# A decoder block with a mixture of experts on one core: weight runs of 8 KB, transposes of strided columns, an input norm on VectorE, and a convolution norm cut into groups of eight transposes

## The chip, the core and the metric

The kernel runs on one core of a Trainium2 chip. The engines of that core are named as in the profile: PE is TensorE, PEld its weight loads, DVE is VectorE, ACT is ScalarE, POOL is GpSimd, and SP is SyncE, whose queue starts most of the DMAs. The metric is the time of one execution on the device, in microseconds (us). Before the change it is 1435.72 us, the median of three runs that lie between 1428.46 and 1436.32 us.

## What is computed

The input `x` has 1024 tokens of 1024 features, all in float32. The block has two mixers on the same normed input, a gate for each, and behind them 32 experts of which every token takes two.

```python
h = rms_norm(x, attn_norm_g)
proj = jnp.matmul(h, w_in)                       # 1024 -> 4608 columns
...
conv_out = conformer_conv(u_conv, ...)           # 31 taps, layer_norm over 512 channels, silu
attn_out = diff_attention(q, k, v, lam, ...)     # 4 heads, causal
merged = (gates[:, :, 0] * jnp.matmul(conv_out, w_conv_out)
          + gates[:, :, 1] * jnp.matmul(attn_out, w_attn_out))
x = x + jnp.matmul(merged, w_out)
h2 = rms_norm(x, ffn_norm_g)
# group of 8 experts by argmax, the two best in it, rows sorted by expert
hid = jax.nn.silu(jnp.matmul(xb, w_g[e])) * jnp.matmul(xb, w_u[e])     # 1024 -> 512
y = jnp.matmul(hid, w_d[e]) * wb[:, None]                              # 512 -> 1024
x = x + scatter_add(y)
```

## The kernel before

Every float32 operand of a large matmul is split into a high and a low part (`split`: ACT copies to the high part, DVE subtracts for the low part, both at lines 93 and 94 of a shared helper), and `mm3` makes three matmuls of each product (lines 98, 99 and 100).

**Prologue and attention (0 to 325 us).** A loop over U goes through 4 heads and 8 blocks of 128 tokens. The order of PE and ACT in it is written out by hand; a string of characters (`plan`) sets where the eight steps of a projection, the transposes of the next token block (`p` and `P`) and the attention steps of earlier blocks stand. In the first eight turns the blocks of `x` are also normed and transposed. SP loads a block into one of four slots of `xts`; ACT sums its squares (`prep_a`), DVE makes 1/sqrt from that (`rsqrt`, lines 65 to 75, ten short instructions); POOL multiplies the block by the norm's weights `gb` (`prep_g`, line 202); DVE multiplies the identity by the 1/sqrt of each token (`prep_s`, line 207); and PE multiplies the block by that diagonal, which transposes and scales it in one (`prep_b`, line 218). The result is split into `hTh` and `hTl`. The low parts of the first head's weights (`wla`) are made by DVE for two chunks and by POOL for two (`wsplit`).

**Merge (325 to 665 us).** Gates are made one after the other, 24 matmuls each (`gate`), with the convolution's taps on DVE between them. The convolution's output is normed over channels in three steps: `norm_stats` (16 transposes, ACT copies them out of PSUM at line 616, DVE makes mean and variance), `norm_silu` (16 transposes back, and for each 512 columns ACT makes a sigmoid at line 635 and an affine copy at line 637) and `norm_split`. Each is done once for each half of the tokens. `merge_conv` puts them between gates by its table `steps`: `norm_stats(0)`, then `norm_silu(0)` with `norm_stats(1)` directly behind it, then `norm_silu(1)`.

**Output projection and routing (665 to 824 us).** For each half of the columns and each token block, PE makes 24 matmuls; DVE adds `x` (line 801); `scaled` multiplies by the second norm's weights on POOL (`uu`, line 815); and ACT's queue stores that to `h2d` in DRAM, from which the experts gather rows. `scaled` permutes in the same step: within every 512 columns element 4p+k goes to place 128k+p, by reads 16 bytes apart. On ACT the store stands ahead of `h2T` (line 865), the copy of a transposed block that PE's logits (`pl`, line 874) need. DVE splits the next block of the merged mixers meanwhile (`ml`, line 94). In the second half, after every second block and at the end, `route` runs a chain of short DVE instructions and small matmuls (`oh`, `ohb`, then `pr` on PE at line 961).

**Experts (824 to 1419 us).** Each of 32 experts has six chunks of 1 MB of weights, which SP loads into a ring of 12 buffers `ra`, with at most five loads in flight (`chunk_dma`). A chunk of the gate or up weights gives each partition one run of 8 KB; a chunk of the down weights gives it two runs of 4 KB. POOL gathers the expert's rows (`gx`, line 1002), PE transposes them (8 transposes in `x_front`, line 1013) and the hidden rows (4 in `hid_t`, line 1041), makes 72 matmuls of 128x512, and POOL adds the result into the output (line 1055).

## Time and profile before

| | |
|---|---|
| median of the runs | 1435.72 us |
| the profiled execution | 1441.21 us, of which the span of instructions is 1439.5 us |
| busy share of the span | PE 94%, PEld 79%, DVE 76%, ACT 55%, POOL 17% |
| granted clock of PE, mean | 0.975 of full speed |
| DMA | 264.81 MB, 184 GB/s over the span |
| chain that ended last | PE 39%, issue 31%, DMA 11%, DVE 7%, POOL 7%, ACT 3% |

The profiled execution is slower than the median by 5.5 us, 0.4%, and 1.7 us of its time lie outside the span. A busy PE is not PE at its peak: its matmuls overlap, and the starts of neighbouring ones say more than their durations.

### The profile page before, as it was taken

To read this page: it belongs to the slowest core of one execution; us is meant where nothing else is said; L and a number is where in the kernel's file an instruction comes from. 1 tells how busy PE (TensorE), PEld (TensorE's weight loads), DVE (VectorE), ACT (ScalarE), POOL (GpSimd) and SP (SyncE) were. 2 spreads that over 40 slices of the span, in tenths; PEclk is the share of its full clock that TensorE was granted. 3 is DMA by queue.
4 is the path that set the end of the run, shared out by engine and by line. 5 is a ranking of instruction groups with operands and counts; after the bars stand their busy time and mean duration, and the time that the engine had idled before them with its cause. 6 is when DMAs were issued, how large, how long until landed. Compare 5 with 4: busy or idle time off the path is not lost.

```text
span 1439.5 us, 18415 instructions
## 1 busy us (share of the span) xinstructions
PE 1349.0 (94%) x6854; PEld 1136.7 (79%) x6854; DVE 1087.7 (76%) x1402; ACT 788.2 (55%) x1109; POOL 240.6 (17%) x349
## 2 busy tenths in 40 slices
PE   5899999999999999899988589999999999999995
PEld 5899999888888888778767468888888887777774
DVE  7776776645789895565575869999998888888893
ACT  4466675653111112531342258888888777777782
POOL 4322121200000000000232211111111212222211
PEclk9999999999999999999997889999999999999997
DMA  5110100102111121043942189999999999999981
GB/s 180 35 45 12 34 18 18 30 27 77 51 44 40 49 59 44 1 130 117 325 158 96 48 297 352 358 371 377 363 370 368 366 368 360 359 361 362 349 326 17
DMA packets 105789, 264.81 MB, mean 184 GB/s; under 512 B 14033, under 2 KB 59234, under 8 KB 89314
## 3 DMA queue, kind: packets, MB, share of 16 engines
q1 hardware_dynamic: 89218, 237.73, 44.8%
q0 software_dynamic: 9216, 16.81, 4.8%
q10 hardware_dynamic: 7264, 9.08, 1.8%
q8 instruction: 55, 0.90, 0.2%
q14 instruction: 36, 0.29, 0.1%
HBM read 255.18 MB, written 25.17 MB: 195 GB/s over the span
## 4 chain that ended last, share of the span: by engine, by line
PE 39%; issue 31%; DMA 11%; DVE 7%; POOL 7%; ACT 3%; POOLq 0%; SPq 0%; ACTq 0%; DVEq 0%
DMA out_dram<-y,idx 8%; PE pg L99 4%; PE pg L98 4%; PE pg L100 4%; POOL out_dram L1055 3%; POOL gx L1002 2%; PE pq L98 2%; PE pq L100 2%; PE pq L99 2%; PE po L363 2%; PE pc L98 2%; PE pc L100 2%; PE pc L99 2%; PE pb L98 2%; PE pb L99 2%
## 5 line engine op out<-in xcount | busy, mean ns | idle before, releaser
L94 DVE TENSOR_TENSOR cl<-ra,ch 128x2048 fp32r<-128x2048 f32 x192 | 436.1, 2289 | 69.6 <-ACT ch L93 69.0
L93 ACT ACTIVATE ch<-ra 128x2048 fp32r<-128x2048 f32 x192 | 365.2, 1920 | 94.7 <-DMA ra<-in_w_gate_e_dram 39.1
L99 PE MATMUL pg<-cl,xh 128*128 128x512 f32 x512 | 203.8, 398 | 4.8 <-DVE cl L94 4.8
L98 PE MATMUL pg<-ch,xh 128*128 128x512 f32 x512 | 203.8, 398 | 3.7 <-ACT ch L93 2.1
L100 PE MATMUL pg<-ch,xl 128*128 128x512 f32 x512 | 201.8, 394 | 0.1
L597 DVE SCALAR_TENSOR_TENSOR ac<-yy,dw,ac 128x1024 f32<-128x1024 f32 x120 | 153.1, 1283 | 2.3
L99 PEld LDWEIGHTS pg<-cl,xh 128*128 128x128 f32 x512 | 96.9, 189 | 27.1 <-DVE cl L94 7.5
L98 PEld LDWEIGHTS pg<-ch,xh 128*128 128x128 f32 x512 | 97.2, 190 | 26.1 <-ACT ch L93 4.1
L100 PEld LDWEIGHTS pg<-ch,xl 128*128 128x128 f32 x512 | 96.9, 189 | 20.5 <-DVE xl L94 0.9
L98 PE MATMUL py<-ch,dh 128*128 128x512 f32 x256 | 103.0, 402 | 1.9 <-ACT dh L93 1.9
L1055 POOL DMA_INDIRECT out_dram<-y,idx x32 | 66.0, 2063 | 226.1 <-ACT y L1054 202.8
L99 PE MATMUL py<-cl,dh 128*128 128x512 f32 x256 | 101.5, 397 | 0.0
L100 PE MATMUL py<-ch,dl 128*128 128x512 f32 x256 | 101.3, 396 | 0.0
L98 PE MATMUL pg<-hTh,whb 128*128 128x512 f32 x256 | 100.1, 391 | 0.0
L100 PE MATMUL pg<-hTh,wlb 128*128 128x512 f32 x256 | 99.8, 390 | 0.0
L99 PE MATMUL pg<-hTl,whb 128*128 128x512 f32 x256 | 99.8, 390 | 0.0
L1002 POOL DMA_INDIRECT gx<-h2d,idx x32 | 53.9, 1685 | 265.5 <-PE pt L1013 226.1
L98 PE MATMUL pq<-wha,hTh 128*128 128x384 f32 x256 | 95.7, 374 | 0.0
L100 PE MATMUL pq<-wha,hTl 128*128 128x384 f32 x256 | 86.8, 339 | 0.8 <-DVE hTl L94 0.8
L93 ACT ACTIVATE whb<-wrb 128x512 fp32r<-128x512 f32 x48 | 30.0, 631 | 104.3 <-PE pg L99 86.1
L99 PE MATMUL pq<-wla,hTh 128*128 128x384 f32 x256 | 86.9, 339 | 0.0
L332 ACT ACTIVATE ee<-sc,mx 128x128 f32<-128x128 f32 (+7 forms) x64 | 47.1, 745 | 22.5 <-DVE mx L330 22.5
(308 smaller groups left out, 2766.3 us busy)
## 6 DMA issues: line engine op xcount, KB each, us to landing
ra<-in_w_gate_e_dram SPq DMA_DIRECT2D x64, 1024.0 KB
ra<-in_w_up_e_dram SPq DMA_DIRECT2D x64, 1024.0 KB
ra<-in_w_down_e_dram SPq DMA_DIRECT2D x64, 1024.0 KB
wrb<-in_w_in_dram SPq DMA_DIRECT2D x32, 256.0 KB
wra<-in_w_in_dram SPq DMA_DIRECT2D x32, 192.0 KB
xts<-in_x_dram SPq DMA_DIRECT2D x8, 512.0 KB
wrb<-in_w_in_dram SPq DMA_DIRECT2D x32, 128.0 KB
wor<-in_w_out_dram SPq DMA_DIRECT2D x8, 512.0 KB
```

The lines of the kernel that those rows point to most:

```text
L93: self.nc.scalar.activation(hi, src, AF.Copy)
L94: self.last_split = (eng or self.nc.vector).tensor_tensor(lo, src, hi.bitcast(F32), op=ALU.subtract).ins
L98: mm(ps, lhsT=lh, rhs=rh, start=first, stop=False)
L99: mm(ps, lhsT=lh, rhs=rl, start=False, stop=False)
L100: mm(ps, lhsT=ll, rhs=rh, start=False, stop=last)
L332: nc.scalar.activation(ee[:, :n], sc[:, :n], AF.Exp, bias=mx, accum_out=s["sm"][qb][:, c:c + 1])
L363: nc.tensor.matmul(po, lhsT=s["at"][j // 4][:, j % 4], rhs=s["V"][j], start=j == 0, stop=j == qb)
L597: nc.vector.scalar_tensor_tensor(ac, yy[:, j:j + T], w(j), ac, op0=ALU.mult, op1=ALU.add)
L1002: self.nc.gpsimd.indirect_dma_start(out=gx, out_offset=None, in_=self.h2d, in_offset=bass.IndirectOffsetOnAxis(ap=idx, axis=0), bounds_che ...
L1055: nc.gpsimd.indirect_dma_start(out=self.out, out_offset=bass.IndirectOffsetOnAxis(ap=idx, axis=0), in_=y, in_offset=None, bounds_check=T - ...
```

## The change

There are four parts.

- **Prologue.** `prep_g` is one DVE instruction, `scalar_tensor_tensor`, that multiplies a block in place by its 1/sqrt and by `gb` (in two pieces for the first two blocks). POOL's multiply and the diagonal are gone, and `prep_b` transposes against the constant identity. There are five slots for `x` instead of four, the order of the first loads differs, and DVE makes the low parts of all four weight chunks. The first two turns of the loop have plans of their own.
- **Convolution norm.** `norm_stats` and `norm_silu` are cut in two, eight transposes each, and each piece stands behind a gate of its own; the last two stand in the loop that projects the convolution's output.
- **Stored rows.** `scaled` is gone: DVE multiplies 512 contiguous columns (`uu`), and rows are stored unpermuted. `x_front` now picks every fourth element of a gathered row, 16 bytes apart, as the operand of its transposes.
- **Down weights.** They are loaded as one run of 8 KB for each partition, and `hid_t` picks every second element, 8 bytes apart, for its transposes.

A fallback loop for experts with more than 128 rows has the same edit of its weight loads; it is not shown.

```diff
@@ -181,9 +181,12 @@
+    def xslot(self, tb):
+        return self.xmisc[:, 3] if tb == 4 else self.xts[:, tb if tb < 4 else tb - 5]
+
...
     def prep_g(self, tb):
-        xt = self.xts[:, tb % 4]
-        self.xg[tb] = xg = xt if tb else self.xmisc[:, 3]
-        self.nc.gpsimd.tensor_tensor(xg, xt, self.gb, op=ALU.mult)
-
-    def prep_s(self, tb):
-        c = (tb % 2) * P
-        self.dg[tb] = dg = self.xmisc[:, 3, c:c + P] if tb else self.xmisc[:, 2, 7 * P:]
-        self.nc.vector.tensor_scalar(dg, self.ident, self.xr[tb], None, op0=ALU.mult)
+        w = D // 2 if tb < 2 else D
+        for c in range(0, D, w):
+            x = self.xslot(tb)[:, c:c + w]
+            g = self.nc.vector.scalar_tensor_tensor(x, x, self.xr[tb], self.gb[:, c:c + w], op0=ALU.mult, op1=ALU.mult)
+        return g.ins
@@ -215,8 +215,7 @@
         for k in range(4):
-            nc.tensor.matmul(pt[:, k], lhsT=self.xg[tb][:, (kk + k) * P:(kk + k + 1) * P], rhs=self.dg[tb],
-                             start=True, stop=True)
+            nc.tensor.transpose(pt[:, k], self.xslot(tb)[:, (kk + k) * P:(kk + k + 1) * P], self.ident)
@@ -402,30 +401,28 @@
             self.xload(0)
+            wload(0, 0)
             nc.sync.dma_start(self.gb, row_bcast(i["attn_norm_g"], D))
-            wload(0, 0)
+            wload(0, 1)
             self.xload(1)
-            wload(0, 1)
             wload(0, 2)
             self.xload(2)
+            self.xload(3)
             wload(0, 3)
-            self.xload(3)
+            self.xload(4)
             self.consts_load()
-            self.xr, self.xg, self.dg = {}, {}, {}
-            self.prep_g(0)
+            self.xr = {}
             self.prep_a(0)
-            self.prep_s(0)
+            with tc.issue_after(self.prep_g(0)):
+                wsplit(0, 0)
+            self.prep_b(0, 0)
+            wsplit(0, 1)
+            self.prep_b(0, 4)
             self.prep_a(1)
+            wsplit(0, 2)
             self.prep_g(1)
...
-            wsplit(0, 3, nc.gpsimd)
+            wsplit(0, 3)
+            self.prep_a(2)
...
@@ -490,12 +485,15 @@
                 plan = "0p12cP3a4qk56Q7" if nxt else "012c3a4qk5Q67"
+                if U < 2:
+                    plan = ("012345p67P", "0123p45P67")[U]
...
                         if U == 0:
+                            self.prep_g(2)
                             self.prep_a(3)
                             self.prep_g(3)
@@ -603,29 +601,32 @@
-    def norm_stats(self, th):
+    def norm_stats(self, th, u):
...
-        for t, zt in enumerate(zs):
+        for t in (2 * u, 2 * u + 1):
...
-    def norm_silu(self, th):
+    def norm_silu(self, th, u):
...
-        for cb in range(NCB):
+        for cb in (2 * u, 2 * u + 1):
@@ -693,26 +694,30 @@
+    def norm_step(self, n, steps):
+        if n in steps:
+            f, th, u = steps[n]
+            f(th, u)
+            if (f, th, u) == (self.norm_silu, 1, 1):
+                self.norm_split(1)
+
     def merge_conv(self, fills, stop, steps):
...
+        order = [(j, th) for j in range(ND - 2) for th in range(2)]
+        order += [(j, th) for th in range(2) for j in (ND - 2, ND - 1)]
+        for n, (j, th) in enumerate(order):
...
+            self.gate(Wg[j], th, s2[th][:, j])
...
+            self.norm_step(n, steps)
+            if (j, th) == (ND - 1, 0):
                 self.norm_split(0)
...
             for j in range(ND):
                 if th == 0 and j + 2 < ND:
                     Wo.append(wload(j + 2))
-                if (th, j) == (0, 2):
-                    self.norm_split(1)
                 pb = self.branch(Wo[j], self.hTh[:, :NCB], self.hTh[:, NCB:], th)
                 sg, mg = s2[th][:, j], self.mg[th][:, j]
                 nc.vector.tensor_tensor(sg, pb, sg, op=ALU.mult)
                 nc.vector.tensor_tensor(mg, mg, sg, op=ALU.add)
+                if th == 0:
+                    self.norm_step(16 + j, steps)
@@ -803,16 +808,12 @@
                 uu = ep.tile([P, 512], F32, name="uu", bufs=2)
-                self.scaled(uu, xt, gb2)
+                nc.vector.tensor_tensor(uu, xt, gb2, op=ALU.mult)
                 nc.scalar.dma_start(self.h2d[sl, ns], uu)
...
-    def scaled(self, uu, xt, gb2):
-        by = lambda a: a.rearrange("t (p k) -> t k p", k=4)
-        self.nc.gpsimd.tensor_tensor(uu.rearrange("t (k p) -> t k p", k=4), by(xt), by(gb2), op=ALU.mult)
@@ -1009,8 +1010,9 @@
             pt = self.ps.tile([P, 4, P], F32, name="pt", tag="T", bufs=2)
+            g = gx[:, k0 * P:(k0 + 4) * P].rearrange("t (p k) -> t k p", k=4)
             for k in range(4):
-                nc.tensor.transpose(pt[:, k], gx[:, (k0 + k) * P:(k0 + k + 1) * P], self.ident)
+                nc.tensor.transpose(pt[:, k], g[:, k], self.ident)
@@ -1038,7 +1040,8 @@
                 c = q * w + k
-                nc.tensor.transpose(pt[:, k], sg[:, c * P:(c + 1) * P], self.ident)
+                g = sg[:, c // 2 * 2 * P:(c // 2 + 1) * 2 * P].rearrange("t (p k) -> t k p", k=2)
+                nc.tensor.transpose(pt[:, k], g[:, c % 2], self.ident)
@@ -1082,10 +1083,9 @@
-        wd = i["w_down_e"][0, e].rearrange("(k p) f -> p k f", p=P)
...
-                [self.chunk_dma(wd[:, k:k + 2]) for k in (0, 2)])
+        wd = i["w_down_e"][0, e].rearrange("(c p k) f -> c p (k f)", p=P, k=2)
+        return ([self.chunk_dma(wg[c], F) for c in range(2)], [self.chunk_dma(wu[c], F) for c in range(2)],
+                [self.chunk_dma(wd[c], D) for c in range(2)])
@@ -1256,8 +1255,9 @@
-        b.merge_conv(6, 4, {4: [(b.norm_stats, 0)], 5: [(b.norm_silu, 0), (b.norm_stats, 1)],
-                            ND - 1: [(b.norm_silu, 1)]})
+        b.merge_conv(6, 4, {8: (b.norm_stats, 0, 0), 9: (b.norm_stats, 0, 1), 11: (b.norm_silu, 0, 0), 12: (b.norm_silu, 0, 1),
+                            13: (b.norm_stats, 1, 0), 14: (b.norm_stats, 1, 1), 17: (b.norm_silu, 1, 0),
+                            19: (b.norm_silu, 1, 1)})
```

What DVE does at the first token block, as it stands in DVE's order (`rr` is the 1/sqrt, `xmisc` the diagonal and, in the new kernel, `gb`). Before:

```order
L75 SCALAR_TENSOR_TENSOR rr<-xn1t,xn1y 128x1
L207 TENSOR_SCALAR xmisc<-ident,rr 128x128
L65 TENSOR_SCALAR xn1v<-ss 128x1
L66 TENSOR_SCALAR xn1y<-xn1v 128x1
L67 TENSOR_SCALAR xn1y<-xn1y 128x1
L68 TENSOR_SCALAR xn1v<-xn1v 128x1
L71 TENSOR_SCALAR xn1t<-xn1y,xn1v 128x1
L94 TENSOR_TENSOR wla<-wra,wha 128x768
L75 SCALAR_TENSOR_TENSOR xn1y<-xn1t,xn1y 128x1
```

After, at the same place, with the buffers' numbers:

```order
L75 SCALAR_TENSOR_TENSOR rr_128<-xn1t_132,xn1y_131 128x1
L206 SCALAR_TENSOR_TENSOR xts_84<-xts_84,rr_128,xmisc_85 128x512 x2
L94 TENSOR_TENSOR wla_146<-wra_92,wha_145 128x768
L94 TENSOR_TENSOR hTl_80<-pt_149,hTh_79 128x4x128
L94 TENSOR_TENSOR wla_157<-wra_96,wha_156 128x768
L94 TENSOR_TENSOR hTl_80<-pt_160,hTh_79 128x4x128
L65 TENSOR_SCALAR xn1v_170<-ss_167 128x1
L66 TENSOR_SCALAR xn1y_171<-xn1v_170 128x1
L67 TENSOR_SCALAR xn1y_171<-xn1y_171 128x1
```

The diagonal has become a multiply of the whole block in two pieces, and two splits of weights and both splits of the transposed first block now stand ahead of the second block's 1/sqrt.

What DVE does where the first routing meets the end of a token block (`wro` takes the sum with `x`, `oh` and `ohb` are the routing's one-hot tables that PE waits for). Before:

```order
L801 TENSOR_TENSOR wro<-wro,px 128x512
L954 CAST ef<-ei 128x4
L966 TENSOR_TENSOR dl<-e_6975 128x2
L972 TENSOR_REDUCE gs<-ge 128x2
L956 TENSOR_TENSOR oh<-io_6342,ef 128x128
L957 TENSOR_TENSOR ohb<-oh 128x64
L969 TENSOR_TENSOR rh<-oh,idm 128x4x32
L971 TENSOR_TENSOR rh<-oh,rr 128x4x32
L979 TENSOR_TENSOR ev<-oh,pr 128x128
L94 TENSOR_TENSOR ml<-mg_4025,mh 128x1024
L981 TENSOR_REDUCE slot<-ev 128x4
L983 TENSOR_TENSOR S<-io_6342,slot 128x512
```

After:

```order
L806 TENSOR_TENSOR wro<-wro,px 128x512
L954 MAX_INDEX ei<-e_6969,off 128x8 x2
L811 TENSOR_TENSOR uu<-wro,gb_6784 128x512
L955 CAST ef<-ei 128x4
L967 TENSOR_TENSOR dl<-e_6969 128x2
L973 TENSOR_REDUCE gs<-ge 128x2
L957 TENSOR_TENSOR oh<-io_6336,ef 128x128
L94 TENSOR_TENSOR ml<-mg_4019,mh 128x1024
L958 TENSOR_TENSOR ohb<-oh 128x64
L970 TENSOR_TENSOR rh<-oh,idm 128x4x32
L972 TENSOR_TENSOR rh<-oh,rr 128x4x32
L980 TENSOR_TENSOR ev<-oh,pr 128x128
```

The multiply `uu` has come into DVE's order ahead of the tables, and the split `ml` of the next block has moved from behind them to between `oh` and `ohb`.

What PE does around the second place of the convolution norm (`pg` is a gate, `pt<-ident,yy` belongs to `norm_silu` and `pt<-ident,ac` to `norm_stats`). Before:

```order
L99 MATMUL pg<-hTl,whb 128x512
L100 MATMUL pg<-hTh,wlb 128x512
L632 MATMUL pt<-ident,yy 128x128 x16
L615 MATMUL pt<-ident,ac 128x128 x16
L98 MATMUL pg<-hTh,whb 128x512
L99 MATMUL pg<-hTl,whb 128x512
```

After, at the first piece of `norm_silu`:

```order
L98 MATMUL pg<-hTh,whb 128x512
L99 MATMUL pg<-hTl,whb 128x512
L100 MATMUL pg<-hTh,wlb 128x512
L633 MATMUL pt<-ident,yy 128x128 x8
L98 MATMUL pg<-hTh,whb 128x512
L99 MATMUL pg<-hTl,whb 128x512
```

Thirty-two transposes between two gates have become eight.

## Rows read from the trace of the kernel before

**Rows 1.** Stretches of the span: from and to in us, length, busy us and instructions of each engine, then PEclk (the granted TensorE clock, 1.00 is full speed), the busy share of the DMA engines, and GB/s.

```profile
20.00:30.00 10.00, 10.00 (x53) 10.00 (x54) 8.61 (x26) 3.58 (x8) 3.70 (x2) 0.74 0.39 122
665.00:824.00 159.00, 137.54 (x717) 111.92 (x715) 101.45 (x263) 44.95 (x84) 39.09 (x21) 0.91 0.47 164
780.00:790.00 10.00, 10.00 (x34) 8.61 (x34) 1.81 (x6) 1.26 (x2) 0.00 (x0) 0.51 0.44 159
824.00:1119.00 295.00, 284.90 (x1331) 236.10 (x1332) 259.36 (x181) 232.09 (x178) 51.33 (x33) 0.97 0.94 353
1119.00:1419.00 300.00, 290.18 (x1340) 233.59 (x1339) 255.69 (x162) 227.43 (x174) 67.07 (x30) 1.00 0.93 338
```

**Rows 2.** Timeline of PE in the first loop turn. Columns here and in the other timelines: start us, duration us, engine, line, operation, out<-in, shape and type, count; in brackets how long the engine sat idle before it and what released it.

```profile
10.25 3.75 PE L218 MATMUL pt<-xmisc 128*128 128x128 f32 x16 [10.25 <-DVE xmisc L207]
...
19.79 2.05 PE L218 MATMUL pt<-xmisc,xts 128*128 128x128 f32 x8 [3.58 <-DVE xmisc L207]
...
28.22 0.33 PE L100 MATMUL pq<-wha,hTl 128*128 128x384 f32 x1
```

**Rows 3.** Timelines of POOL (first two rows) and of DVE (the others) in the same stretch.

```profile
6.85 2.34 POOL L202 TENSOR_TENSOR xmisc<-xts,xmisc 128x1024 f32<-128x1024 f32 x1 [5.00 <-DMA xmisc<-in_attn_norm_g_dram]
...
17.22 2.34 POOL L202 TENSOR_TENSOR xts<-xts,xmisc 128x1024 f32<-128x1024 f32 x1
...
7.10 2.10 DVE L75 SCALAR_TENSOR_TENSOR xn1y<-xn1t,xn1y 128x1 f32<-128x1 f32 x1
...
9.82 0.29 DVE L207 TENSOR_SCALAR xmisc<-ident,rr 128x128 f32<-128x128 f32 x1
...
11.84 2.40 DVE L94 TENSOR_TENSOR wla<-wra,wha 128x768 fp32r<-128x768 f32 x1
...
17.39 2.26 DVE L207 TENSOR_SCALAR xmisc<-ident,rr 128x128 f32<-128x128 f32 x1
```

**Rows 4.** Timeline of PE around the three places of the convolution norm: the last matmul of a gate and the first of the next, and one transpose group between.

```profile
576.39 0.39 PE L100 MATMUL pg<-hTh,wlb 128*128 128x512 f32 x1
...
579.15 0.48 PE L98 MATMUL pg<-hTh,whb 128*128 128x512 f32 x1
...
589.91 0.39 PE L100 MATMUL pg<-hTh,wlb 128*128 128x512 f32 x1
...
592.33 0.66 PE L632 MATMUL pt<-ident,yy 128*128 128x128 f32 x4 [1.15 <-ACT ac L637]
...
598.77 0.47 PE L98 MATMUL pg<-hTh,whb 128*128 128x512 f32 x1
...
609.55 0.39 PE L100 MATMUL pg<-hTh,wlb 128*128 128x512 f32 x1
...
613.73 0.47 PE L98 MATMUL pg<-hTh,whb 128*128 128x512 f32 x1
```

**Rows 5.** Timeline of PE in an expert: eight transposes of a gathered tile, and the matmul behind them.

```profile
969.26 1.04 PE L1013 MATMUL pt<-ident,gx 128*128 128x128 f32 x8
970.06 0.48 PE L98 MATMUL py<-ch,dh 128*128 128x512 f32 x1
```

**Rows 6.** Timelines of DVE, ACT and PEld in one token block of the output projection.

```profile
706.24 3.16 DVE L94 TENSOR_TENSOR ml<-mg,mh 128x1024 fp32r<-128x1024 f32 x1
...
708.78 0.60 ACT L865 ACTIVATE h2T<-pt 128x512 f32<-128x512 f32 x1 [1.51 <-POOL uu L815]
...
709.43 0.97 PEld L874 LDWEIGHTS pl<-wrt,h2T 128*128 128x128 f32 x8 [0.58 <-ACT h2T L865]
```

**Rows 7.** Timeline of DVE in four routings, and a row of PE's waits between 665 and 824 us (engine, tile and line, what it waited for: us in total, times, longest us).

```profile
754.03 2.20 DVE L956 TENSOR_TENSOR oh<-io,ef 128x128 f32<-128x128 f32 x1
...
757.03 1.22 DVE L94 TENSOR_TENSOR ml<-mg,mh 128x1024 fp32r<-128x1024 f32 x1
...
777.15 2.00 DVE L957 TENSOR_TENSOR ohb<-oh 128x64 bf16<-128x64 f32 x1
...
800.52 2.22 DVE L956 TENSOR_TENSOR oh<-io,ef 128x128 f32<-128x128 f32 x1
...
814.23 1.93 DVE L932 TENSOR_TENSOR st<-fss 128x1 f32<-128x1 f32 x1
...
PE pr L961 <- DVE ohb L957: 11.5, 4, 5.6
```

**Rows 8.** Timeline of POOL at the gathers of two neighbouring experts, and waits between 1120 and 1400 us (columns as in the last row of group 7).

```profile
935.11 1.33 POOL L1002 DMA_INDIRECT gx<-h2d,idx  x1 [9.48 <-PE pt L1013]
...
952.84 1.33 POOL L1002 DMA_INDIRECT gx<-h2d,idx  x1 [9.49 <-PE pt L1013]
...
ACT ch L93 <- DMA ra<-in_w_gate_e_dram: 37.2, 21, 5.4
```

**Rows 9.** Two stretches of 3 us in which the ring of weight chunks is filled: the first lies in gate and up chunks, the second in down chunks. Columns as in group 1.

```profile
674.00:677.00 3.00, 3.00 (x15) 2.41 (x14) 0.69 (x1) 1.04 (x1) 0.03 (x1) 1.00 1.02 426
713.00:716.00 3.00, 3.00 (x17) 2.48 (x16) 2.88 (x2) 1.27 (x3) 2.10 (x1) 1.00 1.03 415
```

**Rows 10.** Groups of POOL and of DVE instructions by line and shape: busy us, mean ns of one, then the idle time before them and what ended it.

```profile
L815 POOL TENSOR_TENSOR uu<-wro,gb 128x512 f32<-128x512 f32 x16 | 36.8, 2302 | 106.4 <-DVE wro L801 75.9 <-DVE ef L954 19.2 <-DVE wro L832 11.3
L202 POOL TENSOR_TENSOR xts<-xts,xmisc 128x1024 f32<-128x1024 f32 x7 | 16.5, 2371 | 17.6 <-ACT xmisc L194 17.6
...
L801 DVE TENSOR_TENSOR wro<-wro,px 128x512 f32<-128x512 f32 x15 | 10.3, 684 | 44.8 <-PE px L100 43.3 <-issue 1.5
```

80 lines of the change are left out of this document (30 added, 50 removed).

## The prediction

> **What bounds the kernel now.** I read the stretches first, since the four parts of the change lie in four stages. In [rows 1] the experts take 595 of the 1439.5 us; PE is busy 284.9 of 295 us in their first half and 290.2 of 300 in the second, and DMA is busy 0.93 to 0.94 of the time in both. So PE sets the pace there, with the DMA close behind it: from one gather to the next are 17.73 us in the steady part [rows 8], and later ACT waits for gate chunks, 37.2 us in 21 times [rows 8]. PE idles only 9.8 us in that half. This is the most that faster loads can give there, and the cover that a slower PE finds.
>
> The other stages are not held by PE's work alone. In the output projection PE is busy 137.5 of 159 us at a clock of 0.91 [rows 1], and short waits are to be seen everywhere. The timelines say for what: in [rows 3], [rows 6] and [rows 7] one pattern returns. A DVE instruction that starts beside a multiply of POOL takes 2 us or more, whatever its size: the diagonal takes 0.29 us alone and 2.26 beside POOL [rows 3], the split `ml` 1.22 alone [rows 7] and 3.16 beside it [rows 6]. POOL's multiply is long (2.30 us for 128x512, [rows 10]), and DVE seems to stand until it ends. This change takes these multiplies from POOL.
>
> **The prologue.** PE starts at 10.25 us and starts the second block at 19.79, each time behind the diagonal [rows 2]. Before the first diagonal a step of the 1/sqrt stood 2.10 us beside POOL [rows 3]; without that the 1/sqrt is ready near 7.8 instead of 9.8. The norm's weights landed at 6.85, when POOL started [rows 3]; now a weight chunk of 192 KB goes ahead of them, some 0.5 us at the 415 GB/s of [rows 9], or 1 us with a late start. The multiply of 512 columns costs half of the 1.22 us of `ml`, 0.6 us. The first transpose then starts near 8.9.
>
> The plan of the first turn now has no second block ahead of its matmuls. From 19.79 to 28.39 PE ran without idling [rows 1, 2] and did 8 transposes and 24 matmuls, most of it below the full clock (0.74). The same work and the first eight transposes, 3.4 us at that clock (3.75 us in [rows 2], with the overlap taken off), end at 8.9 + 3.4 + 8.6 = 20.9. Against 28.39 less the three matmuls that belong to the next turn (0.5 us) this is 7 us. In return DVE does eight multiplies of 1.22 us in turns that follow, where PE has little idle time to hide behind; DVE loses its stalls there. I take **−6.5 us**. Bounds: −2, if the last weight chunk or DVE's chain stops the first turn, and −10, if the later turns lose their stalls too.
>
> **The convolution norm.** In [rows 4] PE leaves the gates three times: from 576.39 to 579.15, 589.91 to 598.77, and 609.55 to 613.73. Less one matmul spacing of 0.23 us each, these are 2.5 + 8.6 + 3.95 = 15.1 us for 64 transposes. ACT ends most waits in them (1.15 us behind `ac` at 592.33): it empties PSUM slower than PE fills it. Eight transposes that wait for nothing cost 970.06 − 969.26 = 0.80 us [rows 5], so 64 cost 6.4. Between two pieces now stands a gate of 5.4 us (two gates from 598.77 to 609.55, [rows 4]), and ACT needs half of that for a piece. The gain is 15.1 − 6.4 = **−8.7 us**. What covers ACT's work is the gate; where two pieces have no gate between them (the two in the loop behind the gates) a matmul group of half that length stands instead, and DVE is loaded there as well. Bounds: −6, and −9.
>
> **The stored rows.** Two effects. In the first half of the columns, ACT holds `h2T` back 1.51 us until POOL's multiply ends (the store stands ahead of it on ACT's queue), and PE's logits wait 0.58 us behind that [rows 6], in each of eight blocks: −4.5 us. On DVE the multiply costs 0.69 us, as the addition of the same size [rows 10], and stands ahead of `ml`, which falls from 3.16 to 1.22.
>
> In the routings one DVE instruction stood beside POOL each time, 2.20, 2.00, 2.22 and 1.93 us [rows 7] against 0.3 or less for its like, and PE waited 11.5 us in four times for `ohb` [rows 7]. This stall of 1.9 us goes and the multiply's 0.69 us comes into DVE's chain: −1.2 us four times, about −5. The split `ml` (1.22 us) moves into the first routing's chain and leaves the second's; the two cancel. Behind such a wait PE also runs at half clock, 0.51 from 780 to 790 us [rows 1]. A shorter wait may keep the clock: nothing to −7, of which I take −2.5. Together **−12 us**, bounds −6 and −20.
>
> **The down weights.** The two stretches of [rows 9] both have all DMA engines busy. In gate and up chunks, runs of 8 KB, 426 GB/s move, in down chunks, runs of 4 KB, 415. That is 2.6% on a third of the bytes, 0.9% of some 18 us, or 0.16 us an expert. Where DMA sets the pace it shows at once, and in the first half it keeps the ring full for longer: 30 × 0.16 = **−5 us**. Bounds: nothing, if the pace comes from elsewhere than the runs' length, and −10, all of PE's idle time [rows 1].
>
> **The strided transposes.** No row of this trace has PE read with a stride. Below, the cost is nothing: a transposed tile of eight costs PE 0.1 us each [rows 5], and a weight load beside a matmul may hide a slower read. Above, the nearest row is POOL's `uu`, which reads 16 bytes apart: 2302 ns for 512 columns, where its multiply of 1024 contiguous columns takes 2371 [rows 10], so 1186 for 512, a factor of 1.94. On the eight transposes of gathered rows this is 0.94 × 0.80 = 0.75 us an expert, 24 us in all. I take nothing, since POOL is another engine and its strided instruction also writes and reads a second operand, and keep the upper end for the range.
>
> [...]
>
> **The sum.** −6.5 − 8.7 − 12 − 5 = −32 us. Against the profiled execution's 1441.2 us (a span of 1439.5 and 1.7 around it) this gives 1409. That execution lies 5.5 us above the median of the three runs, 1435.7, against which the sum gives 1403.5. I predict **1408 us**, nearer to the profile, since the shares overlap a little. A measurement of this kernel tells about 0.5%, 7 us, from no change, so "faster" begins below 1428.5.
>
> **The rivals.**
> - *Strided reads slow PE* (those 16 bytes apart, with the factor of [rows 10]). An expert takes 0.75 us more on PE, 18.48 us, 24 us over 32 experts. PE's idle time of 9.8 us takes 10 of it, and the loads' −5 vanishes behind PE: −27 + 14 = −13, 1428 us against the profile, 1423 against the median. For it speaks [rows 10]; against it, that a stationary operand is loaded beside other work (PEld is busy 79%, PE 94%). [...]
> - *Slower: all twelve transposes of an expert are hit, and harder.* At 0.1 us each they cost 1.2 us an expert now. The gains outside the experts, 27 us, and the 10 us of cover are used up at 37/32 = 1.16 us more an expert, so at twice the time for all twelve. At three times it is 77 − 10 − 27 = +40, 1480 us. For it speaks only that neither stride has a row; against it, that the smaller stride skips one element in two.
> - *DVE becomes the bound.* It takes on 16 multiplies of 0.69 and 8 of 1.22 us, 21 us in all, and if its stalls were waits for something else that stays, they don't go. Then the prologue gives −2, the stored rows −3, and the norm −6 with its last pieces late in the loop behind the gates: −16 with the loads, 1425 us. Against it: the pattern of [rows 3] and [rows 7] fits every time.
> - *More than forecast.* If the clock stays up through the routings (−4.5 more) and the loads give all of PE's idle time (−5 more): 1399 us.
>
> **Chances and range.** The forecast (1396 to 1418 by itself) 0.55, strided reads at a price 0.22, DVE as the bound 0.11, slower 0.05, more than forecast 0.07. Taken over the cases, faster by over 0.5% is 0.85 (the forecast, the last case, most of the second and third), within 0.5% 0.09, slower 0.06. The range of 8 in 10 reaches into the second and third cases, from 1393 to 1430 us.
>
> **What would show it.** Right: no POOL multiply before 30 us, the second block's transposes before 20 us, and the first turn over near 21; PE's gates with four pairs of holes of 0.8 us; `ml` at 1.22 us throughout, no DVE instruction of small size above 1 us in the routings, the wait of `pr` below 7 us; PE's window around 780 us above 0.51 of the clock; the period of the experts still 17.73 us, and in the second half less than 9.8 us of idle PE. Wrong: eight transposes of gathered rows that take more than 0.80 us, a period above 17.9 us already before 1100 us, transposes of the norm that wait for DVE or ACT in the loop behind the gates, or a late `wor` (the projection's weights, now all loaded behind the first two blocks of `x`), which would put a hole at the start of the output projection.

## The result and the profile after

The changed kernel takes 1396.26 us, the median of four runs between 1393.02 and 1399.04; the kernel before took 1433.07 beside it. The ratio is 0.9745, with a 95% interval from 0.9705 to 0.9784. The medians differ by 36.8 us. The two profiled executions differ by 46.0 us of span (1439.5 and 1393.5): the one of before was slower than its median and the one of after was not. PE's granted clock, a mean over the span, was 0.975 in the one and 0.986 in the other; the experiments come back to that.

Since the stages follow each other, four marks in the two traces tell where the time came from. A mark is the start of an instruction, in us.

| mark | before | after | gained in the stretch up to it | predicted |
|---|---|---|---|---|
| first matmul of the merge's attention branch (`pb`) | 368.3 | 360.0 | 8.3 | 6.5 (prologue) |
| first matmul of the output projection (`px`) | 670.5 | 653.4 | 8.8 | 8.7 (convolution norm) |
| first gather of an expert's rows (`gx`) | 824.6 | 782.1 | 25.4 | 12 (stored rows) |
| end of the span | 1439.5 | 1393.5 | 3.5 | 5 (loads and strides) |

The marks move between executions of one code. In eleven other kernels that have the changed prologue the first lies between 357.1 and 360.7. In six others with the changed code from `px` to `gx` this stretch takes 128.3 to 132.2 us (128.7 here), and in four others with the same experts the last one takes 610.3 to 612.3 us (611.4 here, 614.9 before).

These are the stretches of the changed kernel that answer to [rows 1], the second from the first `px` to the first `gx`:

```profile
20.00:30.00 10.00, 8.50 (x57) 8.12 (x56) 8.05 (x35) 5.75 (x14) 0.00 (x0) 1.00 0.63 203
653.00:782.00 129.00, 120.39 (x695) 101.52 (x693) 79.56 (x276) 46.54 (x85) 2.31 (x5) 0.97 0.56 202
824.00:1119.00 295.00, 295.00 (x1390) 247.37 (x1389) 265.81 (x185) 239.45 (x183) 47.59 (x33) 1.00 0.96 367
1119.00:1380.00 261.00, 250.77 (x1160) 206.53 (x1158) 216.69 (x139) 192.92 (x149) 43.75 (x25) 1.00 0.87 326
```

The same stretch of the kernel before, by the same marks:

```profile
670.00:825.00 155.00, 132.54 (x695) 107.80 (x693) 99.68 (x260) 45.95 (x84) 39.51 (x22) 0.91 0.48 168
```

Both kernels have 695 recorded matmuls there. Before, PE was busy 132.5 of 155 us at a clock of 0.91; after, 120.4 of 129 at 0.97. Taken by 1 us, the clock is 1.00 in 124 of the 155 windows of before, 0.50 in 24 and between them in seven; after, it is 1.00 in 122 of 129, 0.50 in six and between in one. At 0.50 the matmuls of `px` start 0.43 us apart (780.16 and 780.58 in the trace of before), at 1.00 0.23 us. So such a mean is one of stretches at full clock and at half. As an estimate from these means, a clock of 0.91 over 155 us loses 14 us and one of 0.97 over 129 us loses 4. So of 26 us some 12 were busy time, of which the clock can explain about 10, and some 14 were idle time.

DVE's rows of this stretch by line and shape, and from PE's waits the one that stood in [rows 7]:

```profile
L94 DVE TENSOR_TENSOR ml<-mg,mh 128x1024 fp32r<-128x1024 f32 x15 | 18.3, 1219 | 1.5 <-ACT mh L93 1.5
L811 DVE TENSOR_TENSOR uu<-wro,gb 128x512 f32<-128x512 f32 x15 | 10.3, 687 | 0.3
L957 DVE TENSOR_TENSOR oh<-io,ef 128x128 f32<-128x128 f32 x3 | 0.9, 288 | 0.0
```

```profile
PE pr L962 <- DVE ohb L958: 4.7, 2, 4.4
```

`ml` takes 1.22 us throughout, `uu` 0.69, `oh` 0.29 in every routing, and PE's wait for `ohb` fell from 11.5 to 4.7 us. One small instruction still stood, on two columns, and beside it POOL filled a tile:

```profile
755.63 1.82 DVE L65 TENSOR_SCALAR fn2v<-st 128x2 f32<-128x2 f32 x1
755.59 1.84 POOL L1097 MEMSET gx<- 128x1024 f32 x2 [101.46 <-DVE ml L94]
```

The prologue's PE, where [rows 2] stood: the transposes of the first block, and of the second in two halves.

```profile
9.58 1.94 PE L218 MATMUL pt<-ident,xts 128*128 128x128 f32 x8 [9.58 <-DVE xts L206]
...
17.32 0.63 PE L218 MATMUL pt<-ident,xts 128*128 128x128 f32 x4 [0.78 <-issue]
...
19.77 0.60 PE L218 MATMUL pt<-ident,xts 128*128 128x128 f32 x4
```

The second block is transposed from 17.32 instead of 19.79, and PE did most of the first turn ahead of it.

The counts behind the x show something else. Before, the eight products of the first block with its diagonal are 16 recorded matmuls [rows 2]; now the eight transposes are 8. Here is half a block and the matmul behind it, both at full clock (1.00 from 28 to 30 us), before (first two rows) and after:

```profile
28.39 1.05 PE L218 MATMUL pt<-xmisc,xts 128*128 128x128 f32 x8
29.20 0.42 PE L98 MATMUL pq<-wha,hTh 128*128 128x384 f32 x1
```

```profile
29.01 0.60 PE L218 MATMUL pt<-ident,xts 128*128 128x128 f32 x4
29.36 0.42 PE L98 MATMUL pq<-wha,hTh 128*128 128x384 f32 x1
```

Half a block costs PE 0.35 us instead of 0.81, and over the eight blocks (from the first transpose to the next matmul each time) 16.4 us became 7.2. Up to the first mark, before and after:

```profile
0.00:368.30 368.30, 340.26 (x2162) 313.38 (x2163) 244.66 (x508) 207.67 (x553) 80.04 (x260) 0.99 0.16 47
```

```profile
0.00:360.00 360.00, 332.18 (x2098) 304.36 (x2099) 237.58 (x512) 206.80 (x552) 59.83 (x250) 0.99 0.16 48
```

PE did 64 recorded matmuls less and was busy 8.1 us less. Its idle time is the same, 28.0 and 27.8 us. So in these two traces the gain of the prologue is work that PE no longer has, and none of it is waiting.

The convolution norm, where [rows 4] stood: the last matmul of a gate, a piece of `norm_silu`, and the next gate.

```profile
580.81 0.39 PE L100 MATMUL pg<-hTh,wlb 128*128 128x512 f32 x1
581.04 1.03 PE L633 MATMUL pt<-ident,yy 128*128 128x128 f32 x8
581.83 0.48 PE L98 MATMUL pg<-hTh,whb 128*128 128x512 f32 x1
```

A piece costs 581.83 − 581.04 = 0.79 us and waits for nothing.

In the experts, the gathers that answer to [rows 8], the wait for gate chunks over 290 us (280 in [rows 8]), and the weight loads of the transposes (PEld, by line, mean ns behind the busy us):

```profile
1052.36 1.25 POOL L1003 DMA_INDIRECT gx<-h2d,idx  x1 [9.61 <-PE pt L1015]
1070.20 1.25 POOL L1003 DMA_INDIRECT gx<-h2d,idx  x1 [9.61 <-PE pt L1015]
```

```profile
ACT ch L93 <- DMA ra<-in_w_gate_e_dram: 5.0, 4, 1.6
```

```profile
L1015 PEld LDWEIGHTS pt<-ident,gx 128*128 128x128 f32 x96 | 13.4, 208 | 0.9
L1044 PEld LDWEIGHTS pt<-ident,sg 128*128 128x128 f32 x52 | 8.2, 202 | 1.0
```

And the same weight loads of the kernel before:

```profile
L1013 PEld LDWEIGHTS pt<-ident,gx 128*128 128x128 f32 x104 | 12.1, 140 | 1.7
L1041 PEld LDWEIGHTS pt<-ident,sg 128*128 128x128 f32 x48 | 5.9, 140 | 1.6
```

The period is 17.84 us instead of 17.73. A strided operand takes 202 to 208 ns to load instead of 140, a factor of 1.44 to 1.49, and it is PE's stationary operand. The loads overlap with the matmuls (PEld is busy 81% of the span and PE 95%), and 0.11 us reach the period.

### The profile page after: what moved, and what is told of

Same layout as the page of the kernel before. It is cut to its first block, busy times and chain, and to the rows that moved or that the text cites. A ratio compares the mean times of both kernels' runs of the same rounds, so it can differ in the third digit from the quotient of the medians.

```text
span 1393.5 us, 18240 instructions
## 1 busy us (share of the span) xinstructions
PE 1322.9 (95%) x6790; PEld 1127.0 (81%) x6790; DVE 1058.5 (76%) x1422; ACT 786.0 (56%) x1109; POOL 165.4 (12%) x323
## 4 chain that ended last, share of the span: by engine, by line
PE 43%; issue 33%; DMA 9%; DVE 6%; POOL 6%; ACT 2%; SPq 0%; POOLq 0%; DVEq 0%; ACTq 0%
DMA out_dram<-y,idx 6%; PE pg L100 4%; PE pg L99 4%; PE pg L98 4%; POOL out_dram L1058 3%; POOL gx L1003 3%; PE pq L98 2%; PE pq L100 2%; PE pq L99 2%; PE po L362 2%; PE pb L98 2%; PE pb L99 2%; PE pc L98 2%; PE pc L100 2%; PE pc L99 2%
## 5 line engine op out<-in xcount | busy, mean ns | idle before, releaser
L100 PE MATMUL pg<-hTh,wlb 128*128 128x512 f32 x256 | 99.7, 390 | 0.0
L99 PE MATMUL pg<-hTl,whb 128*128 128x512 f32 x256 | 99.7, 390 | 0.0
L1003 POOL DMA_INDIRECT gx<-h2d,idx x32 | 49.9, 1560 | 296.3 <-PE pt L1015 240.9
L1058 POOL DMA_INDIRECT out_dram<-y,idx x32 | 52.4, 1637 | 225.8 <-ACT y L1057 208.5
L1057 ACT ACTIVATE y<-py,tbl 128x1024 f32<-128x1024 f32 x32 | 35.8, 1118 | 45.1 <-PE py L100 45.1
```

The source lines that it names most:

```text
L99: mm(ps, lhsT=lh, rhs=rl, start=False, stop=False)
L100: mm(ps, lhsT=ll, rhs=rh, start=False, stop=last)
L1003: self.nc.gpsimd.indirect_dma_start(out=gx, out_offset=None, in_=self.h2d, in_offset=bass.IndirectOffsetOnAxis(ap=idx, axis=0), bounds_che ...
L1057: nc.scalar.activation(y, py, AF.Copy, scale=wcol)
L1058: nc.gpsimd.indirect_dma_start(out=self.out, out_offset=bass.IndirectOffsetOnAxis(ap=idx, axis=0), in_=y, in_offset=None, bounds_check=T - ...
```

## The experiments

The kernel before stood beside each group of runs at medians of 1432.9 to 1436.0 us. `px` to `gx` below is the stretch of the third row of the table.

**The stored rows undone.** The changed kernel with its old `scaled` and contiguous transposes of the gathered rows:

```diff
-                nc.vector.tensor_tensor(uu, xt, gb2, op=ALU.mult)
+                self.scaled(uu, xt, gb2)    # POOL, permutes
...
-                nc.tensor.transpose(pt[:, k], g[:, k], self.ident)
+                nc.tensor.transpose(pt[:, k], gx[:, (k0 + k) * P:(k0 + k + 1) * P], self.ident)
```

> The changed kernel with the stored rows as before (POOL multiplies and permutes, the gathered rows are transposed contiguous); the other three parts stay. Theory A, the stored rows are worth the 25 us that lie between the first matmul of the output projection and the first gather, because DVE stands beside POOL's multiply and PE then loses its clock: about 1396 + 25 - 2 (the transposes' stride) = 1419 us, that stretch back at 154 us instead of 129, DVE instructions of over 1.5 us in all four routings and a clock near half after two of them. Rival B, the stored rows are worth the 12 us of the prediction and the other 13 came with another part (loads that start earlier): about 1406 us and a stretch of 141 us.

Measured: a median of 1412.81 us (six runs, 1411.18 to 1420.23), ratio 0.9846 [0.9807, 0.9886]. The profiled execution was the slowest of the six, 1420.2, with a `px` to `gx` of 153.9 us. The stretch of before (154.1) is back with this one part, so all of the 25 us belong to it, in two executions with a low clock (0.975 and 0.978 over the span). In the medians it is worth 1412.8 − 1396.3 = 16.5 us. The executions of this kernel spread over 9 us, those of the changed kernel over 6.

**POOL with contiguous reads.** The multiply goes back to POOL, but it doesn't permute:

```diff
-                nc.vector.tensor_tensor(uu, xt, gb2, op=ALU.mult)
+                nc.gpsimd.tensor_tensor(uu, xt, gb2, op=ALU.mult)
```

> The changed kernel, but the multiply of the stored rows is on POOL with contiguous reads, unpermuted; the transposes stay strided. Theory A (DVE stands until POOL's multiply ends): POOL's instruction falls from 2.3 to about 1.2 us, the stalls of DVE to about 1 us, and about half of the 25 us comes back: 1404 to 1412 us. Rival B (the length of POOL's instruction does not matter, its place in the chain of waits does): as no_rows, less 2 to 3 us.

Measured: 1404.05 us (1402.39 to 1405.97), `px` to `gx` 138.7. By line and shape:

```profile
L94 DVE TENSOR_TENSOR ml<-mg,mh 128x1024 fp32r<-128x1024 f32 x15 | 30.3, 2023 | 2.6 <-ACT mh L93 1.6
L819 POOL TENSOR_TENSOR uu<-wro,gb 128x512 f32<-128x512 f32 x16 | 22.9, 1433 | 103.6 <-DVE wro L806 73.3 <-DVE ef L958 19.0 <-DVE wro L836 11.3
```

POOL's instruction is 0.9 us shorter (1433 ns against the 2302 of [rows 10]), and `ml` stands 0.80 us beside it (2023 ns against 1219) instead of 1.3 (a mean of 2500 ns before). These are means; most of POOL's multiplies took 1.29 us here and 2.11 before. With the instruction's length the cost falls: about half of the loss in the median is gone.

**A multiply of POOL that nobody waits for.** The changed kernel, with DVE's multiply in place, and one more on POOL:

```diff
                 nc.vector.tensor_tensor(uu, xt, gb2, op=ALU.mult)
                 nc.scalar.dma_start(self.h2d[sl, ns], uu)
+                u2 = ep.tile([P, 352], F32, name="u2", bufs=1)
+                nc.gpsimd.tensor_tensor(u2.rearrange("t (k p) -> t k p", k=4),
+                                        by(xt[:, :352]), by(gb2[:, :352]), op=ALU.mult)
```

> The changed kernel, and beside DVE's multiply of the stored rows POOL makes one more of 352 columns, 16 bytes apart, from the same operands into a tile that nobody reads (fifteen in all). Nothing waits for its result. Theory A, DVE stands while POOL's multiply runs, whatever becomes of its result: POOL's instruction takes about 1.6 us, `ml` rises above 1.8 us, single DVE instructions in the routings take 1.3 us or more, and the stretch from the first matmul of the output projection to the first gather grows from 129 to 135 to 140 us: 1403 to 1408 us. Rival B, what cost time before was that the store and the gathered rows waited for POOL's result: the stretch stays within 2 us, 1396.

Measured: 1408.08 us (1404.95 to 1409.47), `px` to `gx` 141.3.

```profile
L94 DVE TENSOR_TENSOR ml<-mg,mh 128x1024 fp32r<-128x1024 f32 x15 | 31.5, 2098 | 1.4 <-ACT mh L93 1.1
L815 POOL TENSOR_TENSOR u<-wro,gb 128x352 f32<-128x352 f32 x15 | 29.1, 1941 | 85.0 <-DVE wro L806 79.2 <-DMA gb<-in_ffn_norm_g_dram 5.8
L811 DVE TENSOR_TENSOR uu<-wro,gb 128x512 f32<-128x512 f32 x15 | 16.8, 1120 | 0.3
```

No result of POOL is used, and still 12 us are lost. DVE's rows show it: `ml` 2.10 instead of 1.22, `uu` 1.12 instead of 0.69, both as means. PE's busy time in the stretch is 4.9 us longer for the same matmuls, at a clock of 0.94 instead of 0.97, and its idle time 7.7 us. The routings' small instructions stayed at 0.3 us, unlike what was expected, since `uu` and `ml` stood in their place. Rival B is out: DVE loses the time beside POOL, whoever needs POOL's result.

**The store on another queue.** The stored rows as before, but their store is issued by SP:

```diff
-                nc.scalar.dma_start(self.h2d[sl, ns], uu)
+                nc.sync.dma_start(self.h2d[sl, ns], uu)
```

> The kernel with the stored rows as before (1412.8 us), but their store is issued on SP's queue and not on ACT's. Theory A, of the 25 us of that stretch only the waits of PE for `h2T` (0.3 to 0.6 us a block) hang on ACT's queue: 3 to 5 us less, the stalls of DVE and the waits for `ohb` unchanged: about 1409 us, the stretch at 149 to 151 us. Rival B, the queue is most of it: below 1403 us. SP now waits with the weights behind it; if that counts, the experts start with an emptier ring and end 2 us later.

Measured: `px` to `gx` 151.0 in the profiled execution, 2.9 us less, and PE waits for `h2T` no longer (3.4 us in the trace of the old rows), apart from 0.5 us at the last block. But other waits took the place of these: for `wro` 5.9 us instead of 1.5, and for `wow` at the start of the output projection 4.1 instead of 1.6. The wait for `ohb` stayed at 10.9 us. PE's idle time in the stretch rose by 3.3 us, and its busy time fell by 6.2 with the same matmuls, at a clock of 0.92 instead of 0.90. So the 2.9 us can't be put down to the queue. The median is 1417.45 us (five runs, 1413.68 to 1428.07), not below the 1412.8. That the queue is most of the loss is out; what it is worth stays open.

**The clock.** The stored rows as before, and twelve matmuls on PE where it waits in three routings:

```diff
+        if G == 2:
+            dm = self.ps.tile([P, 4, P], F32, name="dm", tag="T", bufs=2).rearrange("p a b -> p (a b)")
+            for _ in range(12):
+                nc.tensor.matmul(dm, lhsT=self.dm[0], rhs=self.dm[1], start=True, stop=True)
         pr = self.ps.tile([P, 4, E], F32, name="pr", tag="r2", bufs=1)
```

> The kernel with the stored rows as before (the one that gave 1412.8 us), and twelve more matmuls of 128x512 on PE, whose results nobody reads, ahead of the routing's first small matmuls in three routings, where PE waits. Theory A, part of what the stored rows cost is the clock that PE loses behind these waits, and it also makes the times scatter: no stretch of 10 us below 0.75 between 730 and 790 us, the stretch from the first matmul of the output projection to the first gather 144 to 149 us instead of 154, the median 1404 to 1410. Rival B, the stalls alone cost the time: the stretch stays at 154 or grows by what the twelve matmuls add (up to 2.7 us three times).

Measured: 1417.70 us (1415.74 to 1419.49), `px` to `gx` 152.7. The 70 us with the routings, without the twelve matmuls (first row) and with them (second):

```profile
722.00:792.00 70.00, 60.49 (x311) 49.64 (x310) 47.47 (x172) 16.48 (x33) 16.60 (x9) 0.83 0.25 87
```

```profile
722.00:792.00 70.00, 61.19 (x352) 51.57 (x352) 49.70 (x189) 16.33 (x33) 14.50 (x8) 0.95 0.24 84
```

In nearly the same busy time PE did 352 recorded matmuls instead of 311. The clock rose from 0.83 to 0.95 of full speed, which over 70 us is worth 8 us, and the added matmuls took three times 2.7 us, 8 us as well. So neither number that Theory A gave for the time came, and the stretch stayed near 154, as Rival B had it: the twelve matmuls didn't fit into the waits. What did come of Theory A is the clock (0.83 or more in every 10 us from 732 to 792, against 0.54 from 762 to 772 without the matmuls) and less scatter: 3.8 us between the runs instead of 9.

That scatter follows the clock. The granted clock, a mean over the span, is known for every single run. In the six runs with the old rows it was 0.978 and 0.980 at 1420.2 and 1417.8 us, and 0.983 or 0.984 in the four between 1411.2 and 1413.9 us; 0.006 of 1415 us is 8.5 us. In the 32 runs of the kernel before that stood beside the experiments it was 0.975 or 0.976 in the six slowest (1437.6 to 1441.8 us) and 0.981 to 0.984 in the six fastest (1428.6 to 1430.4 us). The profiled executions of before and of the old rows are among the low ones. So what the stored rows cost in the traces beyond the 16.5 us of the medians (25.3 − 16.5, some 9 us) is about what the clock differs by: 0.978 against the median's 0.983 is 7 us. Why one execution keeps the clock and another doesn't is open.

**DVE permutes.** DVE reads 16 bytes apart in its multiply, and the gathered rows are transposed contiguous:

```diff
-                nc.vector.tensor_tensor(uu, xt, gb2, op=ALU.mult)
+                self.scaled(uu, xt, gb2)    # as before, but nc.vector
```

> The changed kernel, but DVE permutes in its multiply (it reads 16 bytes apart) and the gathered rows are transposed contiguous. Theory A, the stride of 16 bytes costs PE the better part of the 0.11 us an expert by which the period grew (17.84 against 17.73 us): the period falls to about 17.77 and the time by about 2 us, if DVE's strided multiply still takes 0.69 us; if it takes twice that, the routings give about 3 us back. Rival B, the 0.11 us are of another origin (the hidden rows' stride of 8 bytes, or the longer runs of the weights): the period stays at 17.84.

Measured: 1397.23 us (1392.47 to 1398.30), the period 17.77, the experts 1.5 us shorter from the first gather to the end (609.9 against 611.4), `px` to `gx` 131.6 instead of 128.7.

```profile
L820 DVE TENSOR_TENSOR uu<-wro,gb 128x512 f32<-128x512 f32 x16 | 17.8, 1114 | 0.3
```

DVE pays 1114 ns instead of 687 for the distance of 16 bytes. In PE's waits this is seen as 6.9 us for `ohb` instead of 4.7; the stretch itself stays within what the same code varies by (128.3 to 132.2). PE's price of the same permutation, 0.07 us an expert, and DVE's cancel as far as the medians tell.

**The stride doubled.** The gathered rows are transposed 32 bytes apart, with the gate and up chunks cut to match:

```diff
-            g = gx[:, k0 * P:(k0 + 4) * P].rearrange("t (p k) -> t k p", k=4)
+            g = gx.rearrange("t (p k) -> t k p", k=8)
...
-        wg = i["w_gate_e"][0, e].rearrange("(c p k) f -> c p (k f)", p=P, k=4)
+        wg = i["w_gate_e"][0, e].rearrange("(p c k) f -> c p (k f)", c=2, k=4)
```

> The changed kernel with the gathered rows' transposes 32 bytes apart (and the gate and up chunks cut to match, still runs of 8 KB). The period of an expert was 17.735 us with no strides, 17.767 with the four transposes of 8 bytes alone, 17.80 with the eight of 16 bytes alone, 17.84 with both: 9 ns for a transpose at either stride. Theory A, a strided operand costs a fixed 9 ns: the period stays at 17.84 and the time at 1396. Rival B, the cost grows with the distance (doubled from 16 to 32 bytes): a period of 17.91, 2 us more. Rival C, at 32 bytes the read itself sets the pace: 0.4 us and more an expert.

Measured: 1393.81 us (1391.42 to 1397.29), the period 17.775. None of the three theories holds. The weight loads:

```profile
L1015 PEld LDWEIGHTS pt<-ident,gx 128*128 128x128 f32 x96 | 12.6, 192 | 1.0
```

From start to start a group of eight transposes takes 0.79 us contiguous, 0.87 at 16 bytes and 0.81 at 32; four transposes take 0.35 contiguous and 0.385 at 8 bytes. So a stride costs a load some 50 to 70 ns, and a transpose 2 to 10 ns, but at these three distances it doesn't grow (202 ns a load at 8 bytes, 208 at 16, 192 at 32). Why 32 bytes cost less than 16 is open.

**The down weights undone.** Two runs of 4 KB, the hidden rows contiguous:

```diff
-        wd = i["w_down_e"][0, e].rearrange("(c p k) f -> c p (k f)", p=P, k=2)
+        wd = i["w_down_e"][0, e].rearrange("(k p) f -> p k f", p=P)
```

> The changed kernel with the down weights as before (two runs of 4 KB for each partition, the hidden rows transposed contiguous). Theory A, the 8 KB runs are what brought ACT's wait for gate chunks from 37 to 5 us: the waits come back, at least 20 us, and the time grows by 4 to 8 us, 1400 to 1404; the period in the first half falls by a third of 0.11 us to about 17.80. Rival B, the loads are no faster, and the waits shrank because PE takes 0.11 us longer for an expert: the time stays within 2 us of 1396.

Measured: 1397.85 us (1394.32 to 1402.84), the period 17.80, 613.4 us from the first gather to the end against 611.4. The waits came back, the time did not:

```profile
ACT ch L93 <- DMA ra<-in_w_gate_e_dram: 38.8, 21, 5.3
```

The 34 us of ACT's waits come to 2 us at the end, 1 us more than the highest of the five kernels with the changed experts (612.3). The contiguous hidden rows give 0.04 us an expert back at the same time, 1.3 us over 32, so the longer runs by themselves are worth at most some 3 us here. Other kernels with the 8 KB runs have 18.6 (POOL with contiguous reads) or 22.1 us (DVE permutes) of this wait and lose nothing by it either.

**One order for all experts.** In both kernels the order of instructions that the planner writes changes in the last experts: from the 25th gather on, two experts together take 37.85 us (18.93 each), and PE waits once in them. In the changed kernel:

```profile
1243.99 0.50 PE L98 MATMUL pg<-ch,xh 128*128 128x512 f32 x1 [1.58 <-ACT ch L93]
```

The experiment writes the order of the first eighteen experts by hand for all:

```diff
+        with tc.manual_schedule(engines={E_.PE, E_.Activation, E_.DVE}):
+            for e, cur in enumerate(S):
...
+                wu = sum([one(r) for r in cur["raw"][1]], [])
+                p["wd"] = one(p["raw"][2][0])
+                pg = self.proj_f(*cur["x"], cur["wg"])
+                p["dd"] = self.hid_t(p["sg"])
```

> The changed kernel, with the order of the experts' instructions on PE, ACT and DVE written by hand, for all experts as it stands in the first eighteen. Theory A, the pace of the last eight experts (18.93 us, in the kernel before and after alike) is set by another order there, in which PE waits 1.6 us for ACT in every second expert: with one order the period stays at 17.84 to near the end and 6 to 9 us go, 1387 to 1390 us. Rival B, the loads set that pace (the prediction read the second half so): the time stays within 2 us of 1396, and ACT's waits for gate chunks come back, over 20 us.

Measured: 1406.73 us (1403.89 to 1407.98), 10 us slower. The gathers from the 24th on, and the waits over 290 us:

```profile
1161.62 1.12 POOL L1003 DMA_INDIRECT gx<-h2d,idx  x1 [8.62 <-PE pt L1015]
1180.12 1.19 POOL L1003 DMA_INDIRECT gx<-h2d,idx  x1 [8.58 <-PE pt L1015]
1198.82 1.17 POOL L1003 DMA_INDIRECT gx<-h2d,idx  x1 [8.58 <-PE pt L1015]
```

```profile
ACT ch L93 <- DMA ra<-in_w_gate_e_dram: 32.5, 10, 4.0
ACT ch L93 <- DMA ra<-in_w_up_e_dram: 12.1, 13, 1.5
```

Theory A fell: the period rises to 18.5 to 19.3 with the hand order too, and now ACT waits for chunks. That fits loads that set the pace of the last experts, as the prediction read it, and another order there that hides some of their lateness. Rival B's time didn't come either, and some 3 of the 10 us are lost already between the first and the seventh gather, far from the last experts.

**The same with 4 KB runs:**

> The same hand order, with the down weights as before the change (two runs of 4 KB, hidden rows contiguous). Theory A, once the order no longer sets the pace, the loads do, and the 8 KB runs are worth more than the 2 us that they gave in the changed kernel: 3 to 6 us slower than with 8 KB runs. Rival B, the length of the runs changes no load: within 1.5 us of it, or faster by the 1.2 us of the transposes' stride.

Measured: 1407.35 us (1403.60 to 1410.58), no different in the median, with 42.4 and 14.8 us of the two waits and the end 2.8 us later in the trace (624.4 against 621.6 from the first gather). Longer runs help by some 3 us in this trace, too; the times don't tell it from nothing.

**Groups of sixteen.** Two pieces of the convolution norm together behind one gate:

```diff
-            f, th, u = steps[n]
-            f(th, u)
+            f, th = steps[n]
+            for u in range(2):
+                f(th, u)
```

> The changed kernel, but each two pieces of eight transposes of the convolution norm stand together again behind one gate (sixteen in four places). Theory A, a hole is as long as ACT needs to empty what does not fit into two PSUM tiles, as the holes of the kernel before show: 2.5 instead of 1.6 us for the statistics and 3.95 instead of 1.6 for the way back, twice each, 6.5 us in all: about 1403 us. Rival B, the place between gates counts and not the size of the group: within 2 us of 1396.

Measured: 1400.93 us (1399.52 to 1402.27), 4.7 us more in the median. From the first `pb` to the first `px` it takes 299.6 us instead of 293.4, 6.2 us more. The way back of the first half:

```profile
587.19 1.03 PE L633 MATMUL pt<-ident,yy 128*128 128x128 f32 x8
589.38 0.65 PE L633 MATMUL pt<-ident,yy 128*128 128x128 f32 x4 [1.15 <-ACT ac L638]
590.71 0.66 PE L633 MATMUL pt<-ident,yy 128*128 128x128 f32 x4 [0.68 <-ACT ac L638]
```

Eight go through, then PE waits 1.15 and 0.68 us for ACT, as in [rows 4]. Theory A holds to 0.3 us.

**The plans of the first turns undone.**

```diff
-                if U < 2:
-                    plan = ("012345p67P", "0123p45P67")[U]
```

> The changed kernel with the plans of the first two turns as before the change (the second block's transposes stand behind one step and behind three steps of the projection instead of behind six and eight). Theory A, the stalls of DVE beside POOL gave most of the 8 us of the prologue and the plan the smaller part: PE waits near 12 us for the second block, which DVE's chain has ready at about 17 us, so 3 to 5 us are lost of the 8: 1399 to 1401 us. Rival B, the plan is nothing without the stalls: within 1.5 us of 1396.

Measured: 1392.66 us (1392.03 to 1394.50, five runs), ratio 0.9726 [0.9705, 0.9747]; the first `pb` at 357.6.

```profile
18.03 1.08 PE L218 MATMUL pt<-ident,xts 128*128 128x128 f32 x4 [4.55 <-issue]
```

PE waits 4.55 us ahead of the second block, as expected, and ends the first turn 3.5 us later (24.4 against 20.9, by the first copy out of `pq`). By the fourth turn that has turned round: the fourth copy is at 43.86 against 46.45. Two waits of the changed kernel are gone there, 3.0 us in front of the transposes of the fifth block and 1.5 us in front of the third. Theory A fell; B was nearer, and the new plans may even cost 2 us. The shorter transposes are in this kernel too, and the first mark comes as early without the new plans. The intervals of the two ratios overlap, so this kernel can't be called faster than the changed one, though its five runs all lie below the changed kernel's median.

## Why the prediction was right, and where it was not

The time lies in the range, 12 us below the 1408. For the convolution norm the mechanism and the number came as forecast, for the stored rows the mechanism with too small a number. In the prologue the number was right by luck. By the steps:

- **The prologue** was 8.3 us instead of 6.5, within its bounds and little above the scatter of that mark, but not for the reason given. The prediction built its term on waits of DVE beside POOL that go, and took the transposes at their old cost ("the same work"). PE's waits up to the mark did not shrink (28.0 and 27.8 us): those ahead of the second block went, and others came, 3.0 us in front of the fifth block and 1.5 in front of the third. What gave the 8 us is the transposes, 9.3 us less in all, which the prediction had at no change; the x16 in [rows 2] showed that each product with the diagonal was recorded twice. Of the 7.7 us by which the second turn's first matmul starts earlier (20.13 against 27.87), 4.2 are these transposes. The first transpose came at 9.58 and not at 8.9, since the norm's weights landed at 8.72, later than the allowance. What the absence of POOL's multiplies would be worth with the old transposes no run shows; the plans, taken out, lose nothing.
- **The convolution norm** was 8.8 us instead of 8.7, with 0.79 us for each piece. Groups of sixteen give 6.2 of it back in the trace, where the rows of before said 6.5.
- **The stored rows** are the term that was mis-sized: 12 us in the sum, 25.4 in the two traces, 16.5 in the medians. The direction and the mechanism were right, as the spare multiply shows. In the first half of the columns, from block to block, 43.8 us became 41.4 over six blocks (2.4 us; 4.5 was the estimate for eight). The error lies in the routings and behind them. The prediction priced one standing instruction in each, less 0.69 us, and PE's wait for `ohb` did fall by 6.8 us. The clock was taken at −2.5 and its bound at −7; between the two traces it is worth about 10 us, and less in executions of before that kept it better. The upper bound of −20 was too near.
- **The down weights** gave 2 us in the trace against 5 forecast (some 3 without the stride that came with them), less than the times can tell. The row of 2.6% [rows 9] was carried over to the whole of the experts, but ACT's waits behind it are hidden almost entirely: 34 us of them cost 2 or 3. The 3.5 us of the table are more than the runs' length; the rest has no experiment.
- **The strided transposes** cost 0.11 us an expert, at most 3.5 us over 32, against nothing forecast and an upper end of 24. Eight take 0.87 us, so one sign of being wrong (more than 0.80) came true, at a small price; the period, 17.84, stayed under the 17.9 of the other. The rival had only those 16 bytes apart pay, but the load at 8 bytes slows as much (202 ns) as that at 16 (208), and 32 bytes cost less than 16 (192 ns).

The rival in which DVE becomes the bound did not come: DVE's busy time in the stretch from `px` to `gx` fell from 99.7 to 79.6 us, although it took on sixteen multiplies. Nor did the late `wor`.

## What to carry to other kernels

Where DVE instructions of all sizes take as long as a POOL instruction that runs beside them (here one of two columns 1.82 us beside a fill of 1.84; with the old rows `ml` a mean of 2.50 us beside multiplies of 2.32, against 1.22 without them), count every one of them that lies on PE's path, and count the clock that PE loses behind it too (0.54 from 762 to 772 us with the old rows): the same work on DVE can be cheaper than beside it, as here, where `uu` takes DVE 0.69 us and the stored rows gave 16.5 us in the medians. A group of transposes between other matmuls costs only its own time if it fits into the PSUM tiles that stand empty, as eight did here (0.79 us), and what does not fit costs what the engine that empties them needs (1.15 and 0.68 us of waits for ACT with sixteen). Ahead of a forecast on waits, count the instructions of the bound engine before and after: PE's idle time can stay as it was (28.0 and 27.8 us up to the first `pb`) and the kernel be faster all the same. A long total of waits in a view is no price (34 us of ACT's came to 2 us here): change what it waits for, and see what the end does.
